# Three expert groups' gates copied inside SBUF, the first routing chunk's dots moved two steps, 24 instead of 25 groups made ahead

## The chip, the core and the metric

The kernel runs on one NeuronCore of one Trainium2 chip. The metric is the device time of one execution in microseconds (us). The engines are called as the profile calls them: PE (TensorE matmul) and PEld (its weight loads), DVE (VectorE), ACT (ScalarE), POOL (GpSimd) and SP (SyncE, which here only issues DMAs). Each engine works through its own instruction list in order; a DMA that an engine issues runs on the shared DMA engines.

## What is computed

A two-layer decoder trunk on 512 tokens of width 1024. Each layer is a mixer (pooling and retention in layer 0, a gated linear recurrence in layer 1), a residual with layer norm, and then a PEER channel mixer with again a residual and layer norm. The change lies in the PEER part, which is most of the time:

```python
q = (xt @ w_q).reshape(T, PEER_HEADS, 2, PEER_HALF)          # 8 heads
s = jnp.einsum('thpd,hpkd->thpk', q, sub_keys)               # 128 keys a half
s_top, i_top = lax.top_k(s, 16)
cand = s_top[..., 0, :, None] + s_top[..., 1, None, :]       # 16 x 16 pairs
best, pos = lax.top_k(cand, 16)
eid = i_top0 * 128 + i_top1 at pos                           # 16 of 16384 experts
gate = jax.nn.softmax(best)
act = gelu(einsum('td,thkd->thk', xt, u_tab[eid]))
out = einsum('thk,thkd->td', gate * act, v_tab[eid])
```

## The kernel before, in words

Tokens lie in four blocks of 128 (`tb` 0 to 3). For most of them the kernel doesn't gather experts: it multiplies against the whole table of 16384 experts and lets a gate that is zero nearly everywhere pick. The 16384 experts are 128 blocks of 128, and four blocks make a group (`NB = 4`, 32 groups).

- **Dense part, tokens 64 to 383.** `mm1` (L749) multiplies one block of `peer_ut` with 320 tokens (24 matmuls of 320 columns) and puts the gelu into a tile `ge`. `mm2` (L1137) multiplies activation times gate with a block of `peer_v` and adds into six PSUM accumulators (18 matmuls of 512 columns a block). Every matmul is done in three passes on a high and a low half, so each block that streams in (`raw`, L179) is split by ACT (`hi`, L173) and DVE (`lo`, L174).
- **Token block 3** is done by gathering rows: `gather_rounds` (L983) has 128 rounds, each with one row of `u` and one of `v` for all 128 tokens (`row`, L992, an indirect DMA on POOL of 512 KB), a dot product on DVE (L1004), and an accumulation on DVE (L1017).
- **Tokens 0 to 63** have their activations by gathered rows too (`urow`, L745, dots at L109), but their gates times activations are then scattered into a zeroed DRAM buffer `gz` (`add`, L120, an indirect DMA on POOL at L131, each moving 128 values), from where the dense part reads them. `Scatter.place` (L83) makes the indices and issues 16 gathers for a chunk of two heads, `dots` (L106) reduces the rows, `weigh` (L111) makes the products and puts 32 adds into a list, `add` issues some of them. The 16 adds of one head wait until all of the head before have landed (L134). The constant `DOTS` says after which step of which `(chunk, tb)` how many dots are made, `ADDS` how many adds are issued at the three places in a chunk. The adds are kept behind the last gather that was issued before them (L130).

In a PEER layer the stages are these.

1. **Routing** (L725 on). `route_topk` (L771) goes through four chunks of two heads: projections on PE, top 16 on DVE, choice of pairs, for every token block. `route_gates` (L907) then makes, for 8 slices `s` of 32 tokens (tokens 128 to 383), the gate of every expert in `gbuf` [128, 128, 32] by one-hot products, and writes each `gbuf` (2 MB) to DRAM (`gd`, L940, on SP). Meanwhile `lookahead` (L760) does `mm1` for the first `NLA` = 25 groups: each step of routing `yield`s a cost, and for every 2.8 of credit one block is made (L728 to L731). These groups are written to DRAM (`sp`, L768), but for the last two, which are kept in SBUF (`KEEP = 2`). What is left of `lookahead` runs when routing is over (L732).
2. **Experts** (L1020). The remaining 7 groups get their `mm1` here, interleaved among the others. The order begins with one fresh group (`fresh[ROT]`), then the two kept ones. `fetch(n)` (L1041) gets what the n-th group needs: `ge` from `sp`, and the tile `gt` with the gates: slices of tokens 128 to 383 from `gd` (L1053, 512 KB) and those of tokens 0 to 127 from `gz` (L1054 and L142, 256 KB). For n = 0 and 1 the reads are issued on SP and POOL, from n = 2 on ACT. `gz.read` waits until the last head's adds have landed. `high` (L1078) multiplies `gt` by `ge` (L1087, DVE) and rounds it to `ch` (L1091, ACT), `low` makes the rest (L1098, DVE), then `mm2` runs. `front` does an `mm1` six blocks ahead. The gather rounds are spread over the 128 blocks by a cost: 2 for a block whose `mm1` is done there, 1 for another (L1057, L1120).

In `before`, `gt` lies in the pool `ex`, which is opened when routing's pools have been closed, so it takes the addresses that `gbuf` had: the gate reads of the first groups wait for the last write of `gd` for two reasons, the data and the place.

Of the kernel before, what the change touches and what calls it, by code (L numbers as in the profile page):

```python
# [9 lines left out]
F32 = mybir.dt.float32  # L10
# [10 lines left out]
P = 128  # L21
# [8 lines left out]
NB = 4  # L30
# [9 lines left out]
NSD = TD // 32  # L40
NLA = 25
NSZ = 4
# [3 lines left out]
QS = 8  # L46
Y2 = 1.45
YA = 2.3
DOTS = (((0,) * 4, (0, 1, 2, 2), (3, 3, 3, 2), (0,) * 4), ((0,) * 4, (0,) * 4, (1,) * 4, (2,) * 4),
        ((1,) * 4, (0,) * 4, (1,) * 4, (2,) * 4), ((1,) * 4, (0,) * 4, (2,) * 4, (2,) * 4))  # L50
ADDS = ((0, 0, 16), (2, 14), (0, 17), (0, 128))
YB = (1.4, 1.4, 1.4, 4.0)
# [94 lines left out]
class Kern:  # L147
# [547 lines left out]
    def peer(self, layer, xT, hs, out):  # L695
# [3 lines left out]
        with tc.tile_pool(name="pe", bufs=1) as pe:  # L699
# [18 lines left out]
            look = self.lookahead(layer, xT, sp)  # L718
            with tc.tile_pool(name="rk", bufs=1) as rk:
                gz = Scatter(self, rk, layer)  # L720
                kT = rk.tile([P, (TD - P) // GW, 4, GW], F16, name="kT", tag="kT")
                iot = rk.tile([P, P, 2], F16, name="iot", tag="iot")
                nc.gpsimd.iota(iot, pattern=[[1, P], [0, 2]], base=0, channel_multiplier=0,
                               allow_small_or_imprecise_dtypes=True)
                credit = CREDIT0  # L725
                for gen in (self.route_topk(layer, xT, kT, gz), self.route_gates(layer, kT, iot, gd)):
                    for cost in gen:
                        credit += cost  # L728
                        while credit >= 2.8:
                            credit -= 2.8  # L730
                            next(look, None)  # L731
            for _ in look:  # L732
                pass
            g1, b1 = self.load_ln(layer, 1)
            self.experts(layer, xT, hs, gd, gz, sp, lambda tb: self.layernorm(
                tb, hs[tb], g1, b1, None if layer else xT, out if layer else None))
        return xT
# [33 lines left out]
    def route_topk(self, layer, xT, kT, gz):  # L771
        nc, tc, io = self.nc, self.tc, self.io
        with tc.tile_pool(name="rt", bufs=1) as rt, tc.tile_pool(name="rt2", bufs=2) as rt2, \
# [111 lines left out]
            for c in range(4):  # L885
# [11 lines left out]
                for tb in (2, 3):  # L897
                    yield from steps(c, tb, late[tb - 2], YB[c])
                    if c == 0 and tb == 2:
                        gz.weigh(self, rs2)  # L900
                        gz.add(self, ADDS[c][2])
# [5 lines left out]
    def route_gates(self, layer, kT, iot, gd):  # L907
        nc, tc = self.nc, self.tc
        W, L = GW, 2
        Q = W // L  # L910
        with tc.tile_pool(name="rg", bufs=2) as rg:
            b5 = [P, 2, Q, P, L]
            for s in range(NSD - NSZ):
                gbuf = rg.tile([P, P, 32], F32, name="gbuf", tag="gbuf")
                for q in range(32 // W):
# [5 lines left out]

                    oh = rg.tile([P, 2, Q, P, L], F16, name="oh", tag="oh")
                    og = rg.tile([P, 2, Q, P, L], F16, name="og", tag="og")
                    nc.vector.tensor_tensor(oh, iot[:, None, None].broadcast_to(b5), per(0), ALU.is_equal)
# [13 lines left out]
                    if q % 2:  # L938
                        yield 2 * Y2
                nc.sync.dma_start(out=gd[:, :, s].rearrange("g p b t -> p g b t"),  # L940
                                  in_=gbuf.rearrange("p (g b) t -> p g b t", b=NB))

    def lookup(self, pool, pos, i0, i1, thr, i16):
# [76 lines left out]
    def experts(self, layer, xT, hs, gd, gz, sp, norm):  # L1020
        nc, tc, io = self.nc, self.tc, self.io
        with tc.tile_pool(name="ex", bufs=2) as ex, tc.tile_pool(name="ga", bufs=2) as ga:
            ex.tile([P, 48], F32, name="gap", tag="gap")
            accs = [[(self.psC if hf else self.psB).tile([P, 512], F32, name="pC" if hf else "pB",
# [16 lines left out]
            def fetch(n):  # L1041
# [8 lines left out]
                if g < NLA and g not in kept:  # L1050
                    q.dma_start(out=ge, in_=sp[g])
                gt = ex.tile([P, NSD, NB, 32], F32, name="gt", tag="gt", bufs=3)
                q.dma_start(out=gt[:, NSZ:], in_=gd[g])  # L1053
                gz.read(q if n > 1 else nc.gpsimd, gt[:, :NSZ], g)  # L1054
                ges[g] = (ge, gt)
# [219 lines left out]
```

## Time and profile before

| | us |
|---|---|
| median of 3 runs | 2740.01 (2739.19 to 2741.67) |
| the profiled execution | 2737.88 |
| its span, first to last instruction | 2735.9 |
| PE busy in the span | 2675.9 (98%) |
| DVE / ACT / POOL busy | 2417.7 / 1091.4 / 1432.0 |

Times in the rows count from the start of the span, so 2.0 us of the profiled execution lie around it, and the median is 2.1 us above it. Layer 0's PEER part goes from about 125 to 1316 us, layer 1's from about 1540 to the end. In a timeline row the two first numbers are the start and the duration; the bracket at its end is how long the engine was idle before and what ended that. Rows with a q behind the engine (SPq, ACTq) are DMA issues.

### The profile page before, as it was taken

Reading aid. Unit: us, or ns where it says so; the run is one execution under the profiler, and the core shown is the slowest. Engines: PE = TensorE matmul, PEld = TensorE weight load, DVE = VectorE, ACT = ScalarE, POOL = GpSimd, SP = SyncE. Lnnn points to the kernel's source line nnn. Section 1 sums busy time; section 2 is a strip of 40 time slices with the busy share of each in tenths; the row PEclk is TensorE's granted clock in tenths of the full one; section 3 lists DMA queues with packets and bytes.
Section 4 is the critical chain, followed back from the end, with each engine's and each line's share of the span. In section 5 each row is a group of like instructions: output and inputs, shape, how many; then the busy total and the mean of one; then the engine's idle time right before and its main releaser. Section 6 shows DMA issues by size and latency. Waiting matters only on the chain.

```text
span 2735.9 us, 41888 instructions
## 1 busy us (share of the span) xinstructions
PE 2675.9 (98%) x15314; PEld 2376.5 (87%) x15314; DVE 2417.7 (88%) x4684; ACT 1091.4 (40%) x1539; POOL 1432.0 (52%) x929
## 2 busy tenths in 40 slices
PE   9999999999999999999999999999999999999998
PEld 7898999999888888787888889999998888888887
DVE  6678899997899999999798679999996899999999
ACT  3343444654333333333334344344554333333332
POOL 0006777786565666565000016777874566666553
PEclk9999999999999999999999999999999999999999
DMA  6357888799999999999322547889899999999995
GB/s 234 114 201 265 276 279 291 205 264 329 388 412 413 417 416 415 408 417 357 104 79 75 210 160 245 276 270 314 216 269 351 398 414 415 417 415 417 411 416 210
DMA packets 330991, 833.19 MB, mean 305 GB/s; under 512 B 63520, under 2 KB 129568, under 8 KB 330784
## 3 DMA queue, kind: packets, MB, share of 16 engines
q1 hardware_dynamic: 177536, 416.39, 42.9%
q0 software_dynamic: 129344, 336.78, 34.2%
q10 hardware_dynamic: 23904, 77.34, 7.1%
q8 instruction: 120, 1.97, 0.3%
q14 instruction: 87, 0.71, 0.1%
HBM read 747.69 MB, written 82.71 MB: 304 GB/s over the span
## 4 chain that ended last, share of the span: by engine, by line
PE 60%; DVE 12%; issue 11%; DMA 10%; POOL 5%; ACT 0%; DVEq 0%; POOLq 0%; SPq 0%; ACTq 0%
PE pB L1142 9%; PE pC L1142 9%; PE pA L191 9%; PE pA L189 9%; PE pA L190 9%; DMA row<-in_v,eid 7%; POOL row L992 5%; DVE lo L174 3%; PE pC L191 3%; PE pC L189 3%; PE pC L190 3%; DVE h L1017 2%; DMA urow<-in_u,ids 1%; DMA raw<-in_peer_v 1%; PE pB L934 1%
## 5 line engine op out<-in xcount | busy, mean ns | idle before, releaser
L173 ACT CAST hi<-raw 128x1024 fp32r<-128x1024 f32 (+1 forms) x609 | 636.4, 1051 | 959.8 <-PE pC L1142 137.2
L174 DVE TENSOR_TENSOR lo<-raw,hi 128x1024 fp32r<-128x1024 f32 (+1 forms) x609 | 728.7, 1214 | 92.8 <-ACT hi L173 88.6
L131 POOL DMA_INDIRECT gz<-gate,idx x256 | 505.4, 1974 | 155.0 <-issue 72.8
L992 POOL DMA_INDIRECT row<-in_v,eid x256 | 407.9, 1593 | 337.2 <-DVE av L1004 273.8
L191 PE MATMUL pA<-xThi,lo 128*128 128x320 f32 (+2 forms) x1680 | 550.7, 328 | 11.4 <-DVE lo L174 11.4
L189 PE MATMUL pA<-xThi,hi 128*128 128x320 f32 (+2 forms) x1680 | 551.7, 328 | 1.9 <-ACT hi L173 1.9
L190 PE MATMUL pA<-xTlo,hi 128*128 128x320 f32 (+2 forms) x1680 | 549.4, 327 | 0.0
L992 POOL DMA_INDIRECT row<-in_u,eid x256 | 350.4, 1369 | 136.3 <-issue 66.7
L1017 DVE SCALAR_TENSOR_TENSOR h<-row,cf,h 128x1024 f32<-128x1024 f32 x256 | 329.2, 1286 | 44.7 <-DMA row<-in_v,eid 38.5
L191 PEld LDWEIGHTS pA<-xThi,lo 128*128 128x128 f32 x1680 | 316.9, 189 | 28.2 <-DVE lo L174 13.8
L189 PEld LDWEIGHTS pA<-xThi,hi 128*128 128x128 f32 x1680 | 317.0, 189 | 18.0 <-ACT hi L173 2.8
L190 PEld LDWEIGHTS pA<-xTlo,hi 128*128 128x128 f32 x1680 | 316.9, 189 | 15.1
L1004 DVE CUSTOM_DVE_ANT_0 row<-row,x 128x1024 f32<-128x1024 f32 x256 | 310.7, 1217 | 13.1 <-DMA row<-in_u,eid 12.5
L1142 PE MATMUL pB<-lo,ch 128*128 128x512 f32 x768 | 302.0, 393 | 15.7 <-DVE lo L174 15.7
L1142 PE MATMUL pB<-hi,ch 128*128 128x512 f32 x768 | 301.3, 392 | 7.7 <-ACT ch L1091 7.7
L1142 PE MATMUL pB<-hi,cl 128*128 128x512 f32 x768 | 301.2, 392 | 0.0
L1142 PE MATMUL pC<-hi,cl 128*128 128x512 f32 x768 | 301.1, 392 | 0.0
L1142 PE MATMUL pC<-hi,ch 128*128 128x512 f32 x768 | 300.9, 392 | 0.0
L1142 PE MATMUL pC<-lo,ch 128*128 128x512 f32 x768 | 300.9, 392 | 0.0
L745 POOL DMA_INDIRECT urow<-in_u,ids x128 | 158.0, 1235 | 246.6 <-ACT ids L92 190.4
L191 PE MATMUL pC<-xThi,lo 128*128 128x320 f32 x800 | 249.7, 312 | 11.2 <-DVE lo L174 11.2
L189 PE MATMUL pC<-xThi,hi 128*128 128x320 f32 x800 | 250.2, 313 | 0.0
(280 smaller groups left out, 4603.1 us busy)
## 6 DMA issues: line engine op xcount, KB each, us to landing
raw<-in_peer_ut SPq DMA_DIRECT2D x256, 512.0 KB
raw<-in_peer_v SPq DMA_DIRECT2D x256, 512.0 KB
gd<-gbuf SPq DMA_DIRECT2D x16, 2048.0 KB
gt<-gd ACTq DMA_DIRECT2D x60, 512.0 KB
sp<-ge SPq DMA_DIRECT2D x46, 640.0 KB
ge<-sp ACTq DMA_DIRECT2D x46, 640.0 KB
raw<-in_peer_w_q SPq DMA_DIRECT2D x32, 512.0 KB
gz<-zero SPq DMA_DIRECT2D x64, 256.0 KB
```

The costliest lines, as they stand in the source:

```text
L131: d = nc.gpsimd.indirect_dma_start(out=flat, out_offset=bass.IndirectOffsetOnAxis(ap=self.idx[c][:, col], axis=0), in_=gate[:, col], in_of ...
L173: self.nc.scalar.copy(hi, src)
L174: return self.nc.vector.tensor_tensor(lo, src, hi.bitcast(F32), ALU.subtract)
L189: nc.tensor.matmul(ps, ah, bh, start=(first and i == 0), stop=False)
L190: nc.tensor.matmul(ps, ah, bl, start=False, stop=False)
L191: nc.tensor.matmul(ps, al, bh, start=False, stop=(last and i == n - 1))
L745: d = self.nc.gpsimd.indirect_dma_start(out=t, out_offset=None, in_=self.io["u%d" % layer], in_offset=bass.IndirectOffsetOnAxis(ap=ids[:, ...
L934: nc.tensor.matmul(pg[:, sl], oh[:, 0, a, :, b], og[:, 0, a, :, b], start=True, stop=False)
L992: nc.gpsimd.indirect_dma_start(out=t, out_offset=None, in_=io[name], in_offset=bass.IndirectOffsetOnAxis(ap=at, axis=0))
L1004: dot = nc.vector.tensor_tensor_reduce(ur, ur, x, 1.0, 0.0, ALU.mult, ALU.add, av[:, k:k + 1])
L1017: nc.vector.scalar_tensor_tensor(acc, vr, c, acc, ALU.mult, ALU.add)
L1142: nc.tensor.matmul(acc[hf], a[:, ts], b[:, hf * 512:(hf + 1) * 512], start=first and i == 0, stop=last and i == 2)
```

## The change

- **Gates within SBUF.** A pool `gx` is opened between the two routing generators, with three `gt` tiles for the groups that `experts` takes first (`NLA + ROT`, `NLA - 2`, `NLA - 1`). After each slice's `gbuf` has been written out, ACT copies these groups' part (128 x 128 values) into the tiles: 3 copies a slice, 24 a layer. `fetch` then leaves out the read of `gd` for these three, and reads `gz` for all three on POOL (the third was on ACT). The other groups use the same three buffers as before. `gt` no longer lies where `gbuf` was; routing's pool `rk` stays open during `experts`; `oh` and `og` get a pool of their own; a filler tile changes its size.
- **Dots.** The first chunk's 16 dots go from `tb` 1 and 2 to `tb` 2 and 3: the first at `tb` 2's first step instead of `tb` 1's second, the last at `tb` 3's second instead of `tb` 2's fourth. Its `weigh` and first 16 adds follow `tb` 3 instead of `tb` 2.
- **Adds.** In chunk 1, 0 and 16 instead of 2 before the choice and 14 after it; in chunk 2, 16 instead of 17.
- **Groups ahead.** `NLA` 24 instead of 25, and `Y2`, the cost of half a pair of gate steps, 1.4 instead of 1.45.

```diff
-NLA = 25
+NLA = 24
-Y2 = 1.45
+Y2 = 1.4
-DOTS = (((0,) * 4, (0, 1, 2, 2), (3, 3, 3, 2), (0,) * 4), ((0,) * 4, (0,) * 4, (1,) * 4, (2,) * 4),
+DOTS = (((0,) * 4, (0,) * 4, (2, 2, 3, 3), (3, 3, 0, 0)), ((0,) * 4, (0,) * 4, (1,) * 4, (2,) * 4),
-ADDS = ((0, 0, 16), (2, 14), (0, 17), (0, 128))
+ADDS = ((0, 0, 16), (0, 16), (0, 16), (0, 128))
...
+                def routing():
+                    yield from self.route_topk(layer, xT, kT, gz)
+                    self.gx = late.enter_context(tc.tile_pool(name="gx", bufs=1))
+                    self.first = {g: self.gx.tile([P, NSD, NB, 32], F32, name="gt", tag="gt", bufs=3)
+                                  for g in (NLA + ROT, NLA - 2, NLA - 1)}
+                    yield from self.route_gates(layer, kT, iot, gd)
...
-                    if c == 0 and tb == 2:
+                    if c == 0 and tb == 3:
                         gz.weigh(self, rs2)
                         gz.add(self, ADDS[c][2])
...
-        with tc.tile_pool(name="rg", bufs=2) as rg:
+        with tc.tile_pool(name="ro", bufs=2) as ro, tc.tile_pool(name="rg", bufs=2) as rg:
...
                 nc.sync.dma_start(out=gd[:, :, s].rearrange("g p b t -> p g b t"),
                                   in_=gbuf.rearrange("p (g b) t -> p g b t", b=NB))
+                for g, gt in self.first.items():
+                    nc.scalar.copy(gt[:, NSZ + s], gbuf[:, g * NB:(g + 1) * NB, :])
...
-            ex.tile([P, 48], F32, name="gap", tag="gap")
+            ex.tile([P, 88], F32, name="gap", tag="gap", bufs=1)
...
-                gt = ex.tile([P, NSD, NB, 32], F32, name="gt", tag="gt", bufs=3)
-                q.dma_start(out=gt[:, NSZ:], in_=gd[g])
-                gz.read(q if n > 1 else nc.gpsimd, gt[:, :NSZ], g)
+                if g in self.first:
+                    gt = self.first[g]
+                    gz.read(nc.gpsimd, gt[:, :NSZ], g)
+                else:
+                    gt = self.gx.tile([P, NSD, NB, 32], F32, name="gt", tag="gt", bufs=3)
+                    q.dma_start(out=gt[:, NSZ:], in_=gd[g])
+                    gz.read(q, gt[:, :NSZ], g)
```

## Rows read from the trace of the kernel before

**Rows 1.** The page: the engines' busy time, and of the span in 40 equal slices the busy share of the DMA engines in tenths and the GB/s that they moved.
```profile
PE 2675.9 (98%) x15314; PEld 2376.5 (87%) x15314; DVE 2417.7 (88%) x4684; ACT 1091.4 (40%) x1539; POOL 1432.0 (52%) x929
DMA  6357888799999999999322547889899999999995
GB/s 234 114 201 265 276 279 291 205 264 329 388 412 413 417 416 415 408 417 357 104 79 75 210 160 245 276 270 314 216 269 351 398 414 415 417 415 417 411 416 210
```
**Rows 2.** Busy time by stretch: most of layer 0's routing. Columns: the stretch and its length, then busy us of each engine (instructions in brackets), PE's granted clock, the DMA engines' share, GB/s.
```profile
205.00:655.00 450.00, 442.24 (x3149) 424.48 (x3149) 419.07 (x1256) 215.60 (x327) 329.51 (x190) 1.00 0.88 267
```
**Rows 3.** The same view of the experts stage while the gather rounds run: first and second half in layer 0, then in layer 1.
```profile
684.00:960.00 276.00, 276.00 (x1313) 235.55 (x1314) 256.15 (x307) 98.48 (x118) 164.99 (x112) 0.99 1.02 407
960.00:1236.00 276.00, 265.10 (x1247) 225.07 (x1245) 258.99 (x306) 93.43 (x113) 172.90 (x120) 0.98 1.02 414
...
2099.00:2378.00 279.00, 279.00 (x1325) 237.84 (x1326) 258.91 (x310) 99.11 (x119) 171.31 (x113) 0.99 1.02 407
2378.00:2652.00 274.00, 261.68 (x1235) 221.87 (x1233) 256.74 (x304) 92.38 (x112) 171.94 (x120) 0.99 1.03 415
```
**Rows 4.** The chain of work that ended last: twelve `mm2` matmuls in a row at the end of layer 0's experts stage (start, us).
```profile
1295.04 2.72 PE pB L1142 x12
```
**Rows 5.** Who waited for whom (us in total, times, longest): PE over the whole span, and DVE in 960 to 1236 us.
```profile
PE pB L1142 <- ACT ch L1091: 7.7, 2, 4.1
...
DVE h L1017 <- DMA row<-in_v,eid: 11.8, 10, 1.9
```
**Rows 6.** The same view around the first chunk's dots: DVE and PE in 205 to 230 us (layer 0), DVE and PE in 1620 to 1645 us (layer 1).
```profile
DVE urow L109 <- DMA urow<-in_u,ids: 4.9, 3, 2.8
PE pC L191 <- DVE lo L174: 4.1, 1, 4.1
...
DVE urow L109 <- DMA urow<-in_u,ids: 5.2, 3, 2.7
PE pC L191 <- DVE lo L174: 4.7, 1, 4.7
```
**Rows 7.** Timeline of POOL and DVE in layer 0's chunks 0 and 1: the first gather of chunk 0 and its first dot; the first and last of its first 16 adds; the first gather of chunk 1; the end of chunk 0's `tb` 3 (L873); chunk 1's first dot.
```profile
211.47 2.27 POOL L745 DMA_INDIRECT urow<-in_u,ids  x1 [86.02 <-ACT ids L92]
217.95 1.23 DVE L109 CUSTOM_DVE_ANT_0 urow<-urow,xx 128x1024 f32<-128x1024 f32 x1 [2.77 <-DMA urow<-in_u,ids]
...
249.89 1.62 POOL L131 DMA_INDIRECT gz<-gate,idx  x1 [12.50 <-DVE stop L871]
281.13 1.55 POOL L131 DMA_INDIRECT gz<-gate,idx  x1 [0.30 <-issue]
288.73 1.02 POOL L745 DMA_INDIRECT urow<-in_u,ids  x1 [0.30 <-issue]
...
260.15 0.18 DVE L873 CAST itop<-ix 128x64 f16<-128x64 uint32 x1
296.61 1.21 DVE L109 CUSTOM_DVE_ANT_0 urow<-urow,xx 128x1024 f32<-128x1024 f32 x1
```
**Rows 8.** Timeline around chunk 3's gathers, layer 0: the indices (ACT), the one add that POOL issues ahead of them, the first gather.
```profile
424.02 0.42 ACT L92 COPY ids<-eu 64x16 int32<-64x16 int32 x2 [0.30 <-DVE eu L90]
...
424.90 1.57 POOL L131 DMA_INDIRECT gz<-gate,idx  x1 [6.22 <-DVE iy L103]
426.78 1.81 POOL L745 DMA_INDIRECT urow<-in_u,ids  x1 [0.30 <-ACT ge L758]
```
**Rows 9.** Timeline of the passage from routing to experts, layer 0, engine by engine: the last `gbuf` (ACT); its write and the first reads of `gd` (SP); the last add, the first two reads of `gz` (POOL); the first product of gates (DVE); the last matmul of `mm1` and the first of `mm2` (PE).
```profile
655.52 0.61 ACT L936 ACTIVATE gbuf<-pC 128x512 f32<-128x512 f32 x1
...
656.15 0.38 SPq L940 DMA_DIRECT2D gd<-gbuf  x1
667.08 0.80 SPq L1053 DMA_DIRECT2D gt<-gd  x2
...
658.91 1.55 POOL L131 DMA_INDIRECT gz<-gate,idx  x1 [0.30 <-issue]
668.07 0.62 POOL L142 DMA_DIRECT2D gt<-gz  x1 [7.61 <-DMA raw<-in_peer_v]
670.02 0.60 POOL L142 DMA_DIRECT2D gt<-gz  x1
...
679.23 0.82 DVE L1087 TENSOR_TENSOR gt<-gt,ge 128x640 f32<-128x640 f32 x1 [11.09 <-DMA gt<-gz]
...
679.57 0.31 PE L191 MATMUL pA<-xThi,lo 128*128 128x320 f32 x1
683.98 0.80 PE L1142 MATMUL pB<-hi,ch 128*128 128x512 f32 x1 [4.10 <-ACT ch L1091]
```
**Rows 10.** The same passage in layer 1: the first add of the last head, which waits for the head before to land, the last add, the first two reads of `gz` (POOL); the first matmul of `mm2` (PE).
```profile
2032.28 2.14 POOL L131 DMA_INDIRECT gz<-gate,idx  x1 [5.93 <-DMA gz<-gate,idx]
2066.75 1.95 POOL L131 DMA_INDIRECT gz<-gate,idx  x1 [0.30 <-issue]
2083.07 0.62 POOL L142 DMA_DIRECT2D gt<-gz  x1 [14.37 <-DMA raw<-in_peer_v]
2085.02 0.60 POOL L142 DMA_DIRECT2D gt<-gz  x1
...
2098.87 0.50 PE L1142 MATMUL pB<-hi,ch 128*128 128x512 f32 x1 [3.62 <-ACT ch L1091]
```
**Rows 11.** The page's costliest groups: ACT's `hi` (busy us, mean ns of one | idle before).
```profile
L173 ACT CAST hi<-raw 128x1024 fp32r<-128x1024 f32 (+1 forms) x609 | 636.4, 1051 | 959.8 <-PE pC L1142 137.2
```

More of the change, by code (lines that the diff above doesn't have):

```diff
@@ L718, in peer @@
             look = self.lookahead(layer, xT, sp)
-            with tc.tile_pool(name="rk", bufs=1) as rk:
+            with tc.tile_pool(name="rk", bufs=1) as rk, ExitStack() as late:
                 gz = Scatter(self, rk, layer)
@@ L725, in peer @@
                 credit = CREDIT0
[L726 to L736, printed above, removed]
+                def routing():
[4 more added lines that the diff above has]
+                    yield from self.route_gates(layer, kT, iot, gd)
+                for cost in routing():
+                    credit += cost
+                    while credit >= 2.8:
+                        credit -= 2.8
+                        next(look, None)
+                for _ in look:
+                    pass
+                g1, b1 = self.load_ln(layer, 1)
+                self.experts(layer, xT, hs, gd, gz, sp, lambda tb: self.layernorm(
+                    tb, hs[tb], g1, b1, None if layer else xT, out if layer else None))
         return xT
@@ L920, in per @@
                         return v[:, :, :, None, :].broadcast_to(b5)
-                    oh = rg.tile([P, 2, Q, P, L], F16, name="oh", tag="oh")
-                    og = rg.tile([P, 2, Q, P, L], F16, name="og", tag="og")
+                    oh = ro.tile([P, 2, Q, P, L], F16, name="oh", tag="oh")
+                    og = ro.tile([P, 2, Q, P, L], F16, name="og", tag="og")
                     nc.vector.tensor_tensor(oh, iot[:, None, None].broadcast_to(b5), per(0), ALU.is_equal)
```

## The prediction

> **What bounds the kernel now.** I read the page first: PE is busy 98% of the span [rows 1], 60 us of idle in all. Busy share alone doesn't make an engine the limit, so I looked for a stretch where PE certainly works at its pace: twelve matmuls of 512 columns in 2.72 us, 227 ns each [rows 4]. A block of `mm2` is 18 of them, 4.09 us, and 128 blocks are 523 us a layer. The passage after routing gives the price of `mm1`: from the last `gbuf` (655.5) to the last `mm1` matmul (679.9) PE does seven blocks without a gap (three left over from `lookahead`, four of the fresh group), 3.5 us each [rows 9]. By that, the experts stage of layer 0, 24 blocks of `mm1` and 128 of `mm2` from 684.0 on, is 607 us of matmul. So the kernel is bound by PE's work plus the places where PE stands, and a change in it can only move work between stages or take away (or add) standing. Where does PE stand?
>
> In routing PE is busy 442 of 450 us and DVE 419 [rows 2], both nearly full; the largest hole, 4.1 us in layer 0 and 4.7 in layer 1, comes from the first chunk's dots, where DVE waits 4.9 and 5.2 us for gathered rows and the `lo` halves queue behind it [rows 6]. At the passage to experts PE stands 4.1 and 3.6 us for `ch` [rows 5, 9, 10]. In the experts stage it never stands in the first half of the gather rounds and 10.9 and 12.3 us in the second [rows 3], with the DMA engines full all the while: 407 GB/s in the first half, 414 and 415 in the second, no slice of the span above 417 [rows 1, 3]. In that half DVE waits 11.8 us for `v` rows to land [rows 5]. I take this stage to be limited by its bytes: per us of PE work the second half moves 414 x 276 / 265 = 431 KB, more than the 415 that come through.
>
> **Term 1, groups ahead.** One group, four blocks of `mm1`, leaves routing for the experts stage in each layer. Adding up the yielded costs (225.2 in `route_topk`; 46.4 before and 44.8 after in `route_gates`) at 2.8 a block: `route_topk` gets 80 blocks in both, `route_gates` 17 before and 16 after, and the rest after routing is 3 before, none after. PE's work in experts grows by 4 x 3.5 = 14.0 us, in both layers **+28.0**, if nothing absorbs it. The bytes there hardly change: four more 512 KB blocks of `peer_ut`, one 640 KB read of `sp` less, three 512 KB reads of `gd` less, minus 0.13 MB or 0.3 us at 415 GB/s; called zero.
>
> **Term 2, the passage.** In layer 0 the last write of `gd` is issued at 656.15 and the reads go out at 667.08, 10.9 us later, and POOL's first read of `gz` at 668.07 [rows 9]. After the change nothing there needs `gd`. What `gz` needs stays: the last add ends at 660.46 in layer 0, 2068.70 in layer 1. A head's first add waits 5.93 us for the former head to land [rows 10]; with that and the 1.0 us between release and POOL's issue, the first `gz` read goes out at 667.4 (0.7 us earlier than now) in layer 0 and at 2075.6 (7.5 earlier) in layer 1. The add chain itself doesn't move: chunk 3's gathers start 1.9 us sooner since no add stands before them [rows 8], but one add more, 1.95 and 0.30 us, comes behind them.
>
> Then the reads. The second one is issued at 670.02 and DVE starts at 679.23, 9.2 us; `mm2` starts 4.75 later [rows 9]. The three reads of `gd` in front of it go: 1.5 MB at 0.38 to 0.41 MB/us is up to 3.9 us, or nothing if row gathers fill in. I take 1.9 as the middle. So `mm2` starts 2.6 us earlier in layer 0 (0.7 to 4.6) and 9.4 in layer 1 (7.5 to 11.4): **-12.0** (-8.2 to -16.0). PE will stand more than now: it is through with four blocks at 655.5 + 14.0 = 669.5 and then waits to 681.4 in layer 0, about 12 us instead of 4.1; in layer 1 from 2084.7 to 2089.5, about 5.
>
> The trace stands against a rule here: this 256 KB read takes 9.2 us with its wait [rows 9], and I go by that. The Trainium skill, DMA: Bandwidth & Descriptors, section Anatomy of one DMA, gives about 2.0 us plus bytes at 436 GB/s, an estimate of 2.6 us for it. By that estimate the two passages would give -21 instead of -12.
>
> **Term 3, absorbed in experts.** The stage's PE work goes from 607 to 621 us with the same bytes, 2.3% more, so the second halves ask for 431 / 1.023 = 421 KB per us of PE work (425 in layer 1) against 415. If only that half's rate counts, PE stands 276 x (1 - 415/421) = 4 us and 6 instead of 10.9 and 12.3: -13. But the backlog that breaks out in the second half is built in the first, which asks less too; then all 23.2 go. I take most of it, **-20** (-13 to -23), as PE's standing begins only when the slack is used up, half way.
>
> **Term 4, the dots.** The rows land 6.5 us after their issue (211.47 to 217.95) and DVE would come to the first dot after about 220, so most of the 4.9 and 5.2 us go [rows 6, 7]. What is late next: the 16 adds now start after `tb` 3, which ends at 260.15, less the 4.9 saved, 255.3; 1.3 us to the first add and 32.8 for the sixteen [rows 7], so POOL comes to chunk 1's gathers at about 289.6, as late as now (288.73), where DVE is 4 to 5 us ahead and its first dot of that chunk (296.61 now, 292 then) finds its row only at 296. Three of the five us come back there. The two adds taken from before chunk 1's gathers are what keeps it from more. Net **-3** for both layers, between 0 and -8.8.
>
> **Term 5, the rest.** 48 copies on ACT, 128 values a partition: between 0.20 us for 16 values [rows 8] and 1.05 for 1024 [rows 11], about 0.3; 14 us of ACT hidden in an engine busy 216 of 450 [rows 2]. If they hold up the next `gbuf` it would be 0.9 us a slice at most. The third `gz` read on POOL costs 0.9 us of POOL, and group 2 isn't needed for eight blocks. Rows gathered early in experts now lie where the last `gbuf` was and wait for its write, 10.9 us after its issue; they aren't issued sooner now (669). Zero.
>
> Sum: 28.0 - 12.0 - 20 - 3 = -7 to -8 against the profiled 2737.88; the median is 2.1 above that, so 2740.0 - 7.5 = 2732.5, said as **2732**.
>
> **The rivals.**
> *The blocks aren't absorbed.* If PE's standing in experts comes from DVE's order of work and not from bytes, term 3 is near zero and the sum is +13, 2753; slower by more than 0.2% (5.5 us, about what this measurement tells from no change) once the term is under 7. For it: DVE is 94% busy there (259 of 276) and gets four `lo` more. Against: it is 93% busy in the first half, where PE never stands [rows 3].
> *Absorbed by rate alone.* Term 3 at its low end, -13, and everything else as said: 2740, no change.
> *The wait for the reads goes.* If, with an emptier queue, a `gz` read costs no more than its 0.6 us of issue on POOL [rows 9], `mm2` starts at 667.4 + 1.95 + 0.6 + 4.75 = 674.7 in layer 0 and when PE is through, 2084.7, in layer 1: term 2 is -9.3 - 14.2 = -23.5, the sum -18.5, 2721. Against it the 9.2 us of the row; for it that row has the reads of `gd` in front. With the dots' whole gain it would be 2716. By the estimate of 2.6 us from the Trainium skill (DMA: Bandwidth & Descriptors, Anatomy of one DMA) this case would give 2724; no run here shows such a read.
>
> **How the numbers follow.** The forecast (2726 to 2737) 0.43; not absorbed 0.17; absorbed by rate alone, with its neighbours, 0.22; the wait gone 0.18. Range 2716 to 2747: from the third rival with the dots' gain to the high ends of terms 2, 3 and 4 (-8.2, -13, 0 beside 28.0, +7). Faster by over 0.2%: 0.18 and four fifths of the forecast, 0.52; within: 0.22 and the other fifth, 0.30; slower 0.18.
>
> **What would show it.** DVE's first product of gates in layer 0 waiting for `gz`, no longer starting after 680, and PE idle before the first `mm2` for some 12 us there and 5 in layer 1. PE idle in the second half of the gather rounds at 3 us or less a layer, DMA still at 410 GB/s and more. The waits of 4.9 and 5.2 us gone from chunk 0, and one of about 3 us at chunk 1's first dot. Wrong it would be most of all if PE's idle time in experts stayed at 11 and 12 us, or if the adds ended later than 660 and 2069.

## The result, and the profile after

The changed kernel takes 2722.6 us (median of 4 runs, 2722.4 to 2726.4) against 2740.8 for the kernel before (4 runs, 2739.2 to 2743.2): a ratio of 0.9934, 95% interval 0.9919 to 0.9949. It is faster, by 18 us where 7 to 8 were forecast.

The profiled execution of the changed kernel took 2726.4 us (span 2724.6), the longest of its four. Against the profiled 2737.9 of before that is 11.5 us, so the two traces show about two thirds of the difference of the medians; the rest can't be located in them.

The page after (behind the new pool the lines have moved by 7 to 13: `mm2` is L1155, the product of gates L1100, `ch` L1104, a gathered row L1001, the copies L950):

```profile
PE 2674.7 (98%) x15314; PEld 2374.7 (87%) x15314; DVE 2418.8 (89%) x4684; ACT 1101.2 (40%) x1587; POOL 1453.1 (53%) x931
DMA  6357888799999999999322547889799999999995
GB/s 235 108 206 272 273 280 289 208 261 303 412 414 401 414 415 411 414 415 350 104 70 83 208 152 255 273 284 313 217 263 337 413 407 415 413 415 409 415 409 212
```

PE's busy time is within 1.2 us of [rows 1], and no slice of DMA is above 415 GB/s. So the time came from where PE stands, not from less work. Four stretches of the two timelines, each ended by an instruction that both have, cover the spans:

| us (layer 0, layer 1) | before | after | difference |
|---|---|---|---|
| first chunk's indices to the end of the last add | 447.8, 441.4 | 441.4, 440.1 | -6.4, -1.3 |
| end of the last add to the first `mm2` | 23.5, 30.2 | 14.2, 13.4 | -9.3, -16.8 |
| first to last `mm2` | 629.2, 628.1 | 641.3, 638.1 | +12.1, +10.0 |
| everything else | 535.7 | 536.1 | +0.4 |

The differences add up to the span's -11.3. A second trace of the changed kernel (run `again` below, 2726.6 us, also the longest of its runs) gives -7.6, -26.2, +21.5 and +1.1 for the four rows, both layers together, so the split repeats; neither trace holds the rest of the 18 us. The passage in layer 0 after the change, answering to [rows 9]: the last slice's copies (ACT), the last add, the three reads of `gz`, the first row gather (POOL), the first two products of gates (DVE), the last matmul of `mm1` and the first of `mm2` (PE).

```profile
654.89 0.72 ACT L950 COPY gt<-gbuf 128x128 f32<-128x128 f32 x3
...
652.22 1.98 POOL L131 DMA_INDIRECT gz<-gate,idx  x1 [0.30 <-issue]
659.13 1.75 POOL L142 DMA_DIRECT2D gt<-gz  x3 [4.93 <-DMA raw<-in_peer_ut]
668.08 1.32 POOL L1001 DMA_INDIRECT row<-in_u,eid  x1 [7.20 <-issue]
...
665.80 1.57 DVE L1100 TENSOR_TENSOR gt<-gt,ge 128x640 f32<-128x640 f32 x2 [10.76 <-DMA gt<-gz]
...
664.08 0.31 PE L191 MATMUL pA<-xThi,lo 128*128 128x320 f32 x1
668.37 0.80 PE L1155 MATMUL pB<-hi,ch 128*128 128x512 f32 x1 [3.98 <-ACT ch L1104]
```

The first read of `gz` goes out 4.9 us after the last add has ended. It waits for the adds' landing (the row names a load instead): the last add lands at 658.2, and in all nine runs with the copies the first read goes out about 0.9 us after that landing. The other two reads come right behind it, and no row gather stands among them. DVE starts the product as soon as the first read has landed (665.7), 6.7 us after that read's issue; the second lands at 666.5, when the product is already running. The two products run back to back. All this time the last write of `gd` (2 MB, issued at 654.73) is still under way: it lands at 667.3, though nothing in this chain waits for it any more. PE is through with `mm1` at 664.4 and stands 4.0 us, as long as before. Layer 1, answering to [rows 10]:

```profile
2061.97 1.98 POOL L131 DMA_INDIRECT gz<-gate,idx  x1 [0.30 <-issue]
2068.80 1.76 POOL L142 DMA_DIRECT2D gt<-gz  x3 [4.86 <-DMA raw<-in_peer_ut]
...
2075.55 1.56 DVE L1100 TENSOR_TENSOR gt<-gt,ge 128x640 f32<-128x640 f32 x2 [10.77 <-DMA gt<-gz]
...
2077.34 0.80 PE L1155 MATMUL pB<-hi,ch 128*128 128x512 f32 x1 [3.21 <-ACT ch L1104]
```

The experts stage by windows, for [rows 3] (stretch and length, busy us of PE, PEld, DVE, ACT, POOL, PE's granted clock, DMA share, GB/s):

```profile
668.40:960.00 291.60, 291.60 (x1392) 249.32 (x1393) 268.91 (x322) 105.39 (x127) 180.89 (x124) 0.99 1.02 407
960.00:1236.00 276.00, 266.65 (x1274) 227.40 (x1273) 256.12 (x301) 90.27 (x110) 173.53 (x118) 0.98 1.02 413
...
2077.30:2378.00 300.70, 300.20 (x1434) 256.56 (x1435) 277.45 (x331) 106.01 (x128) 184.63 (x127) 0.99 1.02 407
2378.00:2652.00 274.00, 265.48 (x1265) 226.65 (x1264) 255.71 (x300) 92.87 (x113) 170.19 (x117) 0.98 1.02 412
```

PE still stands 9.4 us in the second half in layer 0 and 8.5 in layer 1, where [rows 3] has 10.9 and 12.3. Who waits there, in 960 to 1236 us, for [rows 5] (us in total, times, longest): DVE, then PE.

```profile
DVE h L1026 <- DMA row<-in_v,eid: 14.4, 13, 2.1
DVE row L1013 <- DMA row<-in_u,eid: 5.8, 7, 1.5
...
PE pB L1155 <- DVE lo L174: 7.9, 2, 4.3
PE pA L191 <- DVE lo L174: 1.4, 2, 0.9
```

Rows land late, DVE waits for them in its order, and a `lo` behind them reaches PE late: the same picture as before. DVE's waits for rows are longer than before (20.2 us for 14.6 in this stretch), PE's standing a little shorter. The DMA view of the whole stage in layer 0, before and then after (total and mean rate; issues and KB each):

```profile
DMA packets 69693, 249.52 MB, mean 397 GB/s; under 512 B 7746, under 2 KB 7746, under 8 KB 69653
...
raw<-in_peer_ut SPq DMA_DIRECT2D x22, 512.0 KB
...
row<-in_u,eid POOLq DMA_INDIRECT x121
```

```profile
DMA packets 70745, 253.26 MB, mean 395 GB/s; under 512 B 7856, under 2 KB 7856, under 8 KB 70704
...
raw<-in_peer_ut SPq DMA_DIRECT2D x26, 512.0 KB, 7.5
...
row<-in_u,eid POOLq DMA_INDIRECT x128, 10.1
```

And of the passage, from the last `gbuf` to the first `mm2`, before and after:

```profile
DMA packets 6984, 10.12 MB, mean 363 GB/s; under 512 B 871, under 2 KB 4967, under 8 KB 6982
```

```profile
DMA packets 4870, 4.01 MB, mean 292 GB/s; under 512 B 311, under 2 KB 4407, under 8 KB 4869
```

The shorter passage carries 6 MB less. 1.5 MB of that are the reads of `gd`, which nobody needs any more; but seven row gathers that were issued during the passage before are now issued in the stage, and four blocks of `peer_ut` with them. The stage has 3.7 MB more to bring in, in layer 0 and in layer 1 (246.97 and 250.67 MB), at nearly the same mean rate, 397 and 395 GB/s, 393 and 393. By queue, in layer 0, that is 2.8 MB more on POOL's (the gathers; part of the seven had landed in the stage before too), 1.6 MB more on SP's (the blocks) and 0.65 MB less on ACT's (one read of `sp`). The reads of `gd` inside the stage are 29 in both kernels. Last, the dots, for [rows 6]: DVE in 205 to 235 us (chunk 0), in 290 to 310 (chunk 1), then the same two places in layer 1, 1620 to 1650 and 1700 to 1720.

```profile
DVE urow L109 <- DMA urow<-in_u,ids: 2.0, 3, 1.3
...
DVE urow L109 <- DMA urow<-in_u,ids: 6.8, 1, 6.8
...
DVE urow L109 <- DMA urow<-in_u,ids: 2.3, 3, 1.2
...
DVE urow L109 <- DMA urow<-in_u,ids: 5.4, 1, 5.4
```

### The profile page after: what moved, and what is told of

The parts are those of the page before. It is cut to its first block, busy times and chain, and to the rows that moved or that the text cites. A ratio compares the mean times of both kernels' runs of the same rounds, so it can differ in the third digit from the quotient of the medians.

```text
span 2724.6 us, 41889 instructions
## 1 busy us (share of the span) xinstructions
PE 2674.7 (98%) x15314; PEld 2374.7 (87%) x15314; DVE 2418.8 (89%) x4684; ACT 1101.2 (40%) x1587; POOL 1453.1 (53%) x931
## 4 chain that ended last, share of the span: by engine, by line
PE 46%; DVE 15%; DMA 14%; issue 14%; POOL 10%; ACT 0%; DVEq 0%; POOLq 0%; SPq 0%; ACTq 0%
DMA row<-in_v,eid 10%; PE pA L191 7%; PE pA L189 7%; PE pA L190 7%; POOL row L1001 7%; PE pB L1155 7%; PE pC L1155 6%; DVE lo L174 3%; DMA urow<-in_u,ids 3%; DVE urow L109 2%; POOL gz L131 2%; PE pC L191 2%; PE pC L189 2%; PE pC L190 2%; DVE h L1026 2%
## 5 line engine op out<-in xcount | busy, mean ns | idle before, releaser
L131 POOL DMA_INDIRECT gz<-gate,idx x256 | 513.2, 2005 | 138.4 <-issue 88.4
L1001 POOL DMA_INDIRECT row<-in_v,eid x256 | 404.6, 1581 | 335.8 <-DVE av L1013 263.5
L191 PE MATMUL pA<-xThi,lo 128*128 128x320 f32 (+2 forms) x1712 | 559.1, 327 | 6.4 <-DVE lo L174 6.4
L189 PE MATMUL pA<-xThi,hi 128*128 128x320 f32 (+2 forms) x1712 | 560.4, 327 | 0.8 <-ACT hi L173 0.8
L190 PE MATMUL pA<-xTlo,hi 128*128 128x320 f32 (+2 forms) x1712 | 558.2, 326 | 0.3 <-DVE xTlo L174 0.3
L1001 POOL DMA_INDIRECT row<-in_u,eid x256 | 361.4, 1412 | 135.6 <-issue 74.0
L1155 PE MATMUL pB<-lo,ch 128*128 128x512 f32 x768 | 302.6, 394 | 16.4 <-DVE lo L174 16.4
L1155 PE MATMUL pB<-hi,ch 128*128 128x512 f32 x768 | 302.2, 393 | 7.2 <-ACT ch L1104 7.2
L1155 PE MATMUL pB<-hi,cl 128*128 128x512 f32 x768 | 302.0, 393 | 0.5 <-DVE cl L1111 0.5
L1155 PE MATMUL pC<-lo,ch 128*128 128x512 f32 x768 | 301.7, 393 | 0.0
L1155 PE MATMUL pC<-hi,ch 128*128 128x512 f32 x768 | 301.7, 393 | 0.0
L1155 PE MATMUL pC<-hi,cl 128*128 128x512 f32 x768 | 301.5, 393 | 0.0
L191 PE MATMUL pC<-xThi,lo 128*128 128x320 f32 x768 | 239.2, 311 | 5.5 <-DVE lo L174 5.5
L189 PE MATMUL pC<-xThi,hi 128*128 128x320 f32 x768 | 240.0, 312 | 0.3 <-ACT hi L173 0.3
```

Source lines behind the costliest of these rows:

```text
L131: d = nc.gpsimd.indirect_dma_start(out=flat, out_offset=bass.IndirectOffsetOnAxis(ap=self.idx[c][:, col], axis=0), in_=gate[:, col], in_of ...
L189: nc.tensor.matmul(ps, ah, bh, start=(first and i == 0), stop=False)
L190: nc.tensor.matmul(ps, ah, bl, start=False, stop=False)
L191: nc.tensor.matmul(ps, al, bh, start=False, stop=(last and i == n - 1))
L1001: nc.gpsimd.indirect_dma_start(out=t, out_offset=None, in_=io[name], in_offset=bass.IndirectOffsetOnAxis(ap=at, axis=0))
L1155: nc.tensor.matmul(acc[hf], a[:, ts], b[:, hf * 512:(hf + 1) * 512], start=first and i == 0, stop=last and i == 2)
```

## The experiments

Eleven kernels ran, in three groups, each group on one chip and beside runs of the kernel before (23, 23 and 11 of them; medians 2741.5, 2741.2 and 2741.0). "Difference" is median less median of that group. The changed kernel itself ran in the first group only; kernels of the other two are set against it by their differences.

**The change itself, again.**

> The changed kernel once more, for an interval and a second trace. Expected: 0.993 to 0.994 of before, 2722 to 2724 us; PE idle ahead of the first mm2 about 4 and 3 us; PE idle in the gather rounds 5 to 9 us a layer. The profiled execution shown with the result was 4 us above its other runs; if these 4 us lay in the experts stage, this trace has its mm2 stage shorter by as much.

2723.6 us (2719.7 to 2726.6), ratio 0.9936 (0.9922 to 0.9949), difference -17.9. The result stands, and this is what the others are compared with. Its trace is no shorter than the first: PE stands 5.0 and 3.2 us ahead of `mm2`, and 8.3 and 9.9 us in the stage, so the 4 us by which the profiled execution lay above its other runs were not found.

**25 groups ahead, all else of the change.**

```diff
-NLA = 24
+NLA = 25
-Y2 = 1.4
+Y2 = 1.45
```

> The changed kernel with 25 groups ahead again and Y2 back at 1.45; copies, dots and adds stay changed. Theory A (the gain is the shorter passage to experts, and the moved group costs the experts stage nearly all its 14 us a layer): PE has seven blocks of mm1 after the last gates, so the first mm2 comes about 10 us later a layer and the stage is about 11 us shorter; 2720 to 2726 us, no difference from the change. Theory B (the forecast's: the stage is limited by its bytes and absorbs 10 of the 14 us a layer): slower than the change by 14 to 20 us, 2737 to 2743.

2725.5 us, 0.9944 (0.9931 to 0.9957), difference -16.0. The passage, DVE's first product of gates and PE's first `mm2`:

```profile
665.95 0.82 DVE L1100 TENSOR_TENSOR gt<-gt,ge 128x640 f32<-128x640 f32 x1 [10.64 <-DMA gt<-gz]
...
678.58 0.39 PE L1155 MATMUL pB<-hi,ch 128*128 128x512 f32 x1
```

Here the gates are ready 12.6 us before PE takes them, and PE doesn't stand: it still has its blocks of `mm1`. From the last `gbuf` to `mm2` this kernel takes 23.6 us in both layers and the change 13.7 and 12.9; PE's standing there goes from nothing to 4.0 and 3.2; the experts stage grows from 631.4 and 629.3 us to 641.3 and 638.1, and PE's standing in it falls from 15.3 and 15.9 us to 9.4 and 9.0. So the moved group takes 14 us a layer out of the passage, of which standing puts 3 to 4 back there, and costs 9 to 10 in the stage. Bytes account for more than half of that cost, if the stage runs at its rate: this kernel's stage brings in 250.7 and 248.5 MB, that of the change 253.3 and 250.7; 2.6 and 2.2 MB are 6.5 and 5.6 us at 395 GB/s. The net between the two kernels is 2 us, and the intervals overlap: whether the moved group helps at all is not shown. That is what the first theory expected; the second, the forecast's, expected 14 to 20 us between the two, and is out.

**24 groups ahead alone**, the same two lines on the kernel before.

> The kernel before with 24 groups ahead and Y2 1.4 alone. The passage is still held by the write and the reads of gd, so the first mm2 comes at the same time after the last gates as before, 28 us. Theory A: the stage grows by 10 to 12 us a layer, 2760 to 2764 us. Theory B: it grows by 4, 2747 to 2750.

2745.6 us (12 runs), 1.0012 (1.0002 to 1.0023), difference +4.1, under what either theory expected. The last add and the first two reads of `gz` in layer 0, the first two products, the first `mm2`:

```profile
656.02 1.95 POOL L131 DMA_INDIRECT gz<-gate,idx  x1 [0.31 <-issue]
672.20 0.62 POOL L142 DMA_DIRECT2D gt<-gz  x1 [14.23 <-DMA raw<-in_peer_ut]
673.12 1.03 POOL L992 DMA_INDIRECT row<-in_u,eid  x1 [0.30 <-issue]
674.15 0.60 POOL L142 DMA_DIRECT2D gt<-gz  x1
...
678.95 1.56 DVE L1087 TENSOR_TENSOR gt<-gt,ge 128x640 f32<-128x640 f32 x2 [6.31 <-DMA gt<-gz]
...
680.69 0.80 PE L1142 MATMUL pB<-hi,ch 128*128 128x512 f32 x1 [10.25 <-ACT ch L1091]
```

The read waits 14.2 us though the last add has landed at 661.7: what it waits for is the last write of `gd`, whose place `gt` takes. That was issued at 660.79 and lands at 671.1, 1.1 us before the read. PE, with four blocks fewer of `mm1` to fill the wait, stands 10.2 us at the passage in layer 0 and 9.2 in layer 1 (4.1 and 3.6 before). Without the copies the moved group therefore uncovers the write of `gd`; that the loss is only 4 us is because the stage gives back 3 us of standing a layer and the passage from `gbuf` to `mm2` still shortens by 8, where it had been expected to stay at 28. With 24 groups the product follows the first read (6.7 and 6.5 us after its issue, with the reads of `gd` in front of it), and `mm2` the product by 1.7 us; in the kernel before, the product started when the second read had landed, and two `lo` stood between the products. That part of the shorter passage comes with the moved group, not with the copies.

**The copies undone**: the tiles stay where the change put them, and `gd` is read into them.

```diff
-                for g, gt in self.first.items():
-                    nc.scalar.copy(gt[:, NSZ + s], gbuf[:, g * NB:(g + 1) * NB, :])
...
                     gt = self.first[g]
+                    q.dma_start(out=gt[:, NSZ:], in_=gd[g])
                     gz.read(nc.gpsimd, gt[:, :NSZ], g)
```

> The changed kernel, but the first three groups' gates are read from gd again (into the tiles that no longer lie where gbuf was), with no copies. If the data's way through DRAM holds the passage: the reads start when the last gd write has landed, 11 us after its issue, and take 6 us, so the first mm2 comes 8 us later in each layer and the time is 2736 to 2740 us. If only the place of gt held it: 2722 to 2725.

2738.2 us (12 runs), 0.9991 (0.9981 to 1.0001), difference -3.3: 14.6 us above the change. The passage, SP's last write of `gd` and its first two reads, DVE's first products, PE's first `mm2`:

```profile
651.81 0.38 SPq L947 DMA_DIRECT2D gd<-gbuf  x1
662.62 0.80 SPq L1061 DMA_DIRECT2D gt<-gd  x2
...
668.27 1.56 DVE L1099 TENSOR_TENSOR gt<-gt,ge 128x640 f32<-128x640 f32 x2 [4.61 <-DMA gt<-gd]
...
670.06 0.80 PE L1154 MATMUL pB<-hi,ch 128*128 128x512 f32 x1 [8.59 <-ACT ch L1103]
```

The read of `gd` goes out 10.8 us after its write's issue, as in [rows 9], and the product waits for it. PE stands 8.6 and 8.8 us, 4.6 and 5.6 more than in the change; the first `mm2` comes 18.3 and 18.5 us after the last `gbuf` instead of 13.7 and 12.9. Expected were 8 us a layer; it is about 5, with the time in the range expected all the same. In the two traces, 8.1 us apart, the passages make +10.2 us and the stage +3.2; routing is 4.5 us shorter in this one, which is within what it differs between the traces. Those 10 us, and the slower clock behind a longer stand (below), are what the copies are for. It is the largest single part. That the place alone doesn't hold the passage is shown; what the place alone is worth, no run shows.

**The dots and adds alone**, on the kernel before, and **undone**, in the changed one. The edit of the first, beside `weigh` and the adds moved to `tb == 3`; the second is its reverse:

```diff
-DOTS = (((0,) * 4, (0, 1, 2, 2), (3, 3, 3, 2), (0,) * 4), ((0,) * 4, (0,) * 4, (1,) * 4, (2,) * 4),
+DOTS = (((0,) * 4, (0,) * 4, (2, 2, 3, 3), (3, 3, 0, 0)), ((0,) * 4, (0,) * 4, (1,) * 4, (2,) * 4),
-ADDS = ((0, 0, 16), (2, 14), (0, 17), (0, 128))
+ADDS = ((0, 0, 16), (0, 16), (0, 16), (0, 128))
```

> The kernel before with only the dots and adds of the change. Expected from the trace of the change (its third chunk's indices come 0.7 us later in layer 0 and 2.9 earlier in layer 1, counted from the first chunk's): 2736 to 2740 us. If the dots give what DVE and PE stood at them before: 2731 to 2733.

> The changed kernel with the dots and adds of before. Expected 2723 to 2727 us by the small worth seen in the trace; 2731 if they are worth 9 us. The wait at the first dot of chunk 1 (6.8 and 5.4 us in the change) goes, those at chunk 0 (5 us) come back.

Alone: 2734.5 us (11 runs), 0.9977 (0.9969 to 0.9986), difference -6.7. Undone: 2733.8 us (12 runs), 0.9974 (0.9965 to 0.9983), difference -7.4, so 10.5 less than the change has. In both the edit is worth more than had been expected from the change's trace. In the kernel with the dots alone, last add and first reads of `gz`:

```profile
651.66 1.98 POOL L131 DMA_INDIRECT gz<-gate,idx  x1 [0.31 <-issue]
666.74 0.62 POOL L142 DMA_DIRECT2D gt<-gz  x1 [13.10 <-DMA raw<-in_peer_v]
```

The adds end 6.8 us sooner than before, at 653.6, and the read goes out only 1.3 sooner: it waits for the write of `gd` in the kernel without the copies. That would make the same edit show more inside the change than alone, as the medians have it (10.5 and 6.7), but their intervals meet. The four kernels with 24 groups make a square, though not a clean one (`copies_undone`, the one with dots alone, has the tiles in their new place): neither +4.1, dots -3.3, copies -7.4, both -17.9. Both together give 3.1 us more than the two steps added up (4.1 - 7.4 - 11.5 = -14.8); the intervals, 2.5 to 4 us to either side, are too wide to call that surplus measured.

**Half of the accumulation left out, then half of the bytes too.** The first makes the accumulation of the gathered `v` rows on 512 of 1024 columns; the second gathers only these columns, from a table of half the width (256 KB a row instead of 512). In both, half of token block 3's expert output is not computed.

```diff
-                nc.vector.scalar_tensor_tensor(acc, vr, c, acc, ALU.mult, ALU.add)
+                w = slice(0, D // 2)
+                nc.vector.scalar_tensor_tensor(acc[:, w], vr[:, w], c, acc[:, w], ALU.mult, ALU.add)
```

> The changed kernel with the accumulation of gathered v rows done for the first 512 of 1024 columns only (so token block 3 is half computed): 0.6 us less of DVE in each of 128 rounds, 77 us a layer, with the same bytes moved. If DVE's work holds PE in the gather rounds: PE's standing there (9.3 and 8.5 us in the change's trace) goes, 2705 to 2710 us. If bytes hold it: 2718 to 2724, PE idle as before.

> As less_dve, and the v rows are gathered at half their width, 256 KB instead of 512 KB: 33.5 MB less a layer at the same DVE work. If bytes hold the stage: PE idle in the gather rounds goes to under 2 us a layer, the DMA rate falls from 410 to some 360 GB/s, 12 to 18 us faster than less_dve. If DVE held it: the same time as less_dve.

2714.6 us (0.9909, 0.9895 to 0.9923) and 2697.9 us (0.9844, 0.9832 to 0.9857): 9 and 25 us less than the change, by the differences (-26.6 and -43.3). The first lies between what the two theories expected, the second where the one that goes by bytes has it. (DVE's busy time in layer 0's stage fell by 60 us, not 77.) Second half of layer 0's gather rounds, first kernel, then second:

```profile
960.00:1236.00 276.00, 271.09 (x1304) 231.69 (x1303) 229.48 (x305) 90.61 (x112) 148.83 (x120) 0.99 1.03 413
```

```profile
960.00:1236.00 276.00, 276.00 (x1338) 236.91 (x1337) 237.24 (x313) 98.23 (x118) 161.30 (x122) 1.00 0.97 371
```

And DVE's waits for rows in the same stretch of the first kernel:

```profile
DVE h L1027 <- DMA row<-in_v,eid: 24.3, 22, 2.5
DVE row L1013 <- DMA row<-in_u,eid: 16.1, 13, 2.9
```

DVE works 26.6 us less, waits 20.2 us longer for the same rows at the same 413 GB/s, and PE still stands 4.9 us there. With fewer bytes PE doesn't stand at all (0.0 and 0.5 us in the whole stage), and the stage takes 626.3 and 624.9 us: that is its length by PE alone. The stage of the change is 15.0 and 13.2 us over it, that of before, with 14.0 less work, 16.9 and 17.2. So the bytes are the larger part of what sets the pace, and DVE's work has a share: without a tenth of DVE's work alone, a third of the excess goes (5.4 of 15.0, 4.6 of 13.2 us); without a quarter of the rows' bytes as well, all of it. No run takes the bytes away with DVE's work whole, so what the bytes alone are worth is not shown.

**Two attempts at a better kernel**, on the change, alone and together: the second chunk's dots later, and another pace of the gather rounds.

```diff
-... ((0,) * 4, (0,) * 4, (1,) * 4, (2,) * 4),
+... ((0,) * 4, (0,) * 4, (0, 0, 2, 2), (2,) * 4),
```

```diff
-                return 2.0 if i + AHEAD < NE and order[(i + AHEAD) // NB] >= NLA else 1.0
+                return 2.3 if i + AHEAD < NE and order[(i + AHEAD) // NB] >= NLA else 1.0
```

> The change, with the second chunk's first dots two steps later (0, 0, 2, 2 at its token block 2 instead of 1, 1, 1, 1). Theory A: the gathered rows of this chunk are late there because POOL comes to them only after the first chunk's 16 adds, so DVE's waits of 6.8 and 5.4 us at its first dot go, PE's standing in routing falls from 5.7 to about 3.5 us a layer, and the slower clock behind a stand goes with it: 3 to 8 us less than the change, 2715 to 2720. Theory B: DVE is so full in routing that what it doesn't wait for here it waits for later (second or third chunk's rows, or the choice of pairs that follows): waits change place, 2721 to 2725.

> The change, with a block whose mm1 is done in the experts stage counted 2.3 instead of 2 in the pacing of the gather rounds, which makes the bytes per us of PE work about equal on both kinds of blocks. Theory A: PE stands in that stage where demand is locally over what the DMA engines bring, so evening it out takes most of the 9 us of standing a layer away, with the slower clock behind it: 2705 to 2716. Theory B: over the second half as a whole the demand is over what comes (413 GB/s through, 14 and more us of DVE's waits for v rows), so the stand moves and stays 8 to 10 us a layer: 2720 to 2726.

> Both edits, the second chunk's dots two steps later and 2.3 for a block with mm1. They act in different stages, so each theory expects the sum of what the two do alone, within 2 us: 2697 to 2712 if both gain, 2720 to 2726 if neither does.

2720.9 us (0.9925, 0.9913 to 0.9937), 2722.5 (0.9933, 0.9922 to 0.9945) and 2722.3 (0.9928, 0.9916 to 0.9940), beside the change's 0.9934 and 0.9936: none can be told from it. For the pace the first theory is out (2705 to 2716); for the dots the time lies between the two theories. With later dots the wait at chunk 1's first dot shrinks from 6.8 to 4.2 us in layer 0 and from 5.4 to 4.5 in layer 1 but doesn't go, and PE's standing in routing goes from 5.8 and 5.7 us to 4.1 and 5.7. With the other pace PE's waits in layer 0's stage are these:

```profile
PE pB L1155 <- DVE lo L174: 9.0, 4, 3.8
PE pB L1155 <- ACT ch L1104: 3.6, 1, 3.6
```

Two long stands for `lo` (7.9 us in all) have become four (9.0): the standing moved and stayed, as the second theory has it.

## Why the prediction came out as it did

The sign and the main mechanism were right: gates kept in SBUF bring `mm2` forward, a moved group costs PE work in experts. The size was less than half of the measured one (7 to 8 us for 18). By the profiled executions:

| | predicted | measured |
|---|---|---|
| term 1, PE work moved into experts | +28.0 | +27.6 |
| term 2, the passage | -12.0 | -26.1 |
| term 3, absorbed in experts | -20 | -5.5 |
| term 4, dots and adds (routing) | -3 | -7.7 |
| term 5, the rest | 0 | +0.4 |
| sum | -7.0 | -11.3 |

Terms 2 and 3 each missed by some 14 us, with opposite signs. That the sum comes within 5 us of the traces is luck in good part; the time lay below the forecast (2726 to 2737), where the third rival stood.

**Term 1** was right. PE's busy time in the stage is its length less PE's standing: 617.7 and 615.7 us before, 631.9 and 629.1 after, +14.2 and +13.4.

**Term 2** had the releaser right and every size too long. The first read was to wait 6.9 us after the adds; it waits 4.9. The product was to follow the second read, 1.95 + 7.3 us behind the first one's issue; it follows the first, by 6.7. From the product to `mm2` I kept 4.75 us; it takes 2.6, because the two products run back to back (before, two `lo` of 2.35 us together stood between them). With 2.0, 2.6 and 2.2 us these make up the 6.8 us by which layer 0's passage came out shorter than forecast (14.2 for 20.9). The last two came with the 24 groups, as `ahead24_alone` has them without the copies. PE doesn't stand 12 and 5 us either, but 4.0 and 3.2: `mm2` comes that much sooner, and PE is through with `mm1` 9.7 us after the last `gbuf`, under three blocks where I counted four. Why the read still takes 6.7 us with no read of `gd` in front, the nine runs with the copies show. In fifteen of their eighteen passages the first read goes out while the last write of `gd` is under way, and lands 6.0 to 8.3 us after its issue. In three the adds end so late that it goes out as that write lands or after, and then it takes 3.1 us. One of them is layer 0 of the changed kernel with the dots undone, where the write lands at 669.8:

```profile
669.91 1.76 POOL L142 DMA_DIRECT2D gt<-gz  x3 [6.80 <-DMA gd<-gbuf]
...
673.05 0.83 DVE L1100 TENSOR_TENSOR gt<-gt,ge 128x640 f32<-128x640 f32 x1 [13.93 <-DMA gt<-gz]
```

So the copies take the write out of the chain, but its 2 MB still share the DMA engines with the read that follows; no run takes the write away, and what else moves then is not separated. The Trainium skill's estimate of 2.6 us (DMA: Bandwidth & Descriptors, Anatomy of one DMA) is near those 3.1 and well under the 6.7.

**Term 3** is the step that failed, and in it one sentence: "the same bytes". Term 1's count set three reads of `gd` less against four blocks more and called the difference zero; but those reads lay in the passage, ahead of the stage, which has 29 of them before and after. And the passage that got shorter had carried bytes too: 10.1 MB before, 4.0 after. Row gathers that were done while PE worked off its blocks now come when `mm2` runs; I had seen that they aren't issued sooner than before (668.1, and 669.0 then), and not that `mm2` now starts by then. The stage therefore has 3.7 MB more in each layer, 2.8 of it gathered rows, and at its rate of 395 and 393 GB/s that is 9.5 and 9.4 us, of the 12.1 and 10.0 by which it grew. That is an account and not a test: the rate itself differs by 2% between kernels (390 to 398 GB/s with full rows), and in `ahead24_alone` the stage grows by 10.7 and 10.9 us for 2.3 and 2.7 MB more. My view that the stage is limited by its bytes was borne out in the main (with less DVE work and fewer bytes PE doesn't stand), with a share for DVE. Had I kept to it, the passage's gain would have had to be paid partly in the stage. PE's standing fell by 2.1 us in layer 0 and 3.4 in layer 1 instead of 10 each, so the sign that I had named for being wrong (11 and 12 us of standing as before) came close. The rival "the blocks aren't absorbed" set 7 us as the point under which the kernel would be slower; the term did come under it, with DVE's work a part of the reason and not all of it, and the kernel was faster since terms 2 and 4 were larger.

**Term 4** was right in where the waits go: chunk 0's fall from 4.9 and 5.2 to 2.0 and 2.3, and a new one comes at chunk 1's first dot. That is 6.8 and 5.4 us instead of 3, since the sixteen adds took 37.7 us rather than 32.8 and chunk 1's gathers start at 292.4, not 289.6. PE hardly feels it: its waits for `lo` in layer 0 from 213 to 320 us are 2.4 us where they were 4.3. What I had left out is the adds' end. "The add chain itself doesn't move" was wrong in layer 0, where it ends 7.0 us sooner after chunk 3's indices. 2.1 of that is chunk 3's gathers starting sooner, as forecast; 3.1 is that its adds took 160.6 us (80 of them) instead of 163.7 (79), 1.7 the pauses between them. The adds' durations differ between executions (155.8 to 162.3 us for 80, 156.7 to 163.7 for 79, in these kernels), so only the first part can be put down to the edit. That the edit is worth more than 3 us the timed runs show; where all of it comes from stays open.

**Term 5** was right: 48 copies at 0.30 us, and `gbuf` isn't held up.

The rival nearest to the measured time, "the wait for the reads goes" (2721), was near it by a sum of errors: the wait for the first read is still 6.7 us.

## What to carry to other kernels

Where data that is written out is wanted back at once, a copy within SBUF takes the write's landing out of the chain (14.6 us here, for 14 us of an engine with room). But ask what the chain waits for next: the write's bytes still move beside the reads that follow. A part can also look wrong by itself: the moved group cost 4 us without the copies and with them nothing that these intervals show. Before you shorten a stretch, add up the bytes that it carries: if the next stage is limited by its transfers, what no longer fits into the stretch is paid there.

## What the runs showed of the hardware

A stand of PE costs more than its length. Around one in layer 0 of the changed kernel, by windows (columns as above; the clock is the figure before the last two):

```profile
1227.50:1231.80 4.30, 0.03 (x2) 0.01 (x1) 3.80 (x7) 0.00 (x0) 2.34 (x2) 0.89 1.02 409
1231.80:1237.00 5.20, 5.20 (x12) 4.12 (x13) 5.20 (x7) 0.00 (x0) 3.54 (x2) 0.50 0.99 355
1237.00:1245.00 8.00, 8.00 (x35) 6.53 (x34) 8.00 (x10) 3.48 (x4) 3.65 (x4) 0.96 1.00 384
```

After 4.3 us without a matmul the granted clock is 0.50, that is 1.2 instead of 2.4 GHz, for the next 5.2 us and then full again: 5.2 x 0.5 + 8.0 x 0.04 = 2.9 us are lost on top of the 4.3. After the stand at the passage it is 0.50 for 3.6 us and 0.69 for 4.0, 3.0 us. It shows in the sums: in the kernel with fewer bytes the standing in the stage falls by 9.4 and 8.5 us, the stage by 15.0 and 13.2. The Trainium skill, TensorE: Matmul & The Clock Gate, section Why this matters for your kernels, warns that an idle gap between bursts of matmuls puts the clock back to half; the trace agrees. I had priced standing by its idle time alone, so 4 us of it were worth about 7.

A read that nothing holds in its queue can still take twice as long: 256 KB issued on POOL landed 3.1 us after issue when the 2 MB write before it had landed or was just landing (three passages), and 6.0 to 8.3 us after issue while that write was under way (fifteen).
